# Building the next block's right factors inside the running block, by way of HBM, and last down weights in the up weights' buffers

## Chip, core and metric

The kernel runs on one core of a Trainium2 chip. The metric is the device time of one execution in microseconds (us), lower is better. Before the change it is 3266.54 us, the median of three runs (3254.4, 3266.54 and 3267.34).

The core's engines work side by side, each through its own instructions in order: TensorE (PE in the profile) multiplies matrices, VectorE (DVE) and GpSimd (POOL) do elementwise arithmetic, ScalarE (ACT) does activations and copies, and SyncE (SP) issues most transfers between HBM and the on-chip memory. They meet through semaphores.

## The reference, cut to the part that matters

One layer over 2048 tokens of width 1024 in float32: three token mixers side by side on a normalised input, a projection back that is added to `x`, and then a gated feed-forward part with a convolution of three taps over time. The change lies in the last line only.

```python
h = rms_norm(x, mix_norm_g[l])
...
x = x + jnp.concatenate([ya, yb, yc], axis=-1) @ w_out[l]
h = rms_norm(x, ffn_norm_g[l])
x = x + conv_glu_ffn(h, w_up[l], conv_w[l], conv_b[l], w_down[l])

def conv_glu_ffn(h, w_up, conv_w, conv_b, w_down):
    gate, val = jnp.split(h @ w_up, 2, axis=-1)
    gp = jnp.pad(gate, ((0, 0), (CONV_W - 1, 0), (0, 0)))
    conv = conv_b
    for i in range(CONV_W):
        conv = conv + gp[:, i:i + t] * conv_w[i]
    return (jax.nn.silu(conv) * val) @ w_down
```

`w_up` is 1024 x 5632 and `w_down` 2816 x 1024.

## The kernel before

The feed-forward part (lines 1246 to 1382) runs over three blocks of tokens, `BL`: 688, 680 and 680 tokens, each treated as two halves of n = 344 or 340 columns. Within a block a loop runs over the NF = 22 groups `fi` of 128 hidden units.

**Products in parts.** Every float32 matrix is split into a rounded high part and a rest (`split`, lines 142 to 144: a copy on ScalarE makes the high part, a subtraction on VectorE, or on GpSimd for down weights, the rest), and a product is three matmuls: high by high, high by rest, rest by high.

**Up projection.** `ffn_up` computes gate and value for both token halves by a scheme of seven products in the place of eight (Strassen's, in Winograd's form). The left factors are sums and differences of weight quarters: `up_w` loads two raw tiles of 512 KB (pool `raw`, three buffers), GpSimd makes four `S` tiles, and for each product ScalarE and VectorE split one left factor into a buffer `wu` (four buffers). The right factors, `Bs`, are seven tiles `B0` to `B6` made once for a block: `build` takes the rows j and j + 4 of `x` (eight rows of 128 features, scaled by two instructions of VectorE, line 1164), forms four sums and differences on GpSimd (lines 1169 to 1172) and splits seven tiles. Over j that is 8 scalings, 16 subtractions on GpSimd and 28 splits for a block. One product is 12 matmuls, a group `fi` 84. VectorE then adds seven results out of PSUM, two convolution taps (line 1314), the product with the value (line 1316) and the split of `hid`.

**Down projection.** After every second `fi` the two groups that are ready are multiplied by their down weights (`ffn_down`): 16 steps of six matmuls, and one addition into `acc` on VectorE for each (line 1338). Down weights (`down_w`) have two buffers `wd`, filled by a ScalarE copy and a GpSimd subtraction of 1024 columns.

**The end of a block.** After the last `fi` four groups are left: two rounds of down projection, 32 steps. The buffers of the right factors are free once the last up group has read them, so `build` for the next block stands here: one step of it after each of the 32 down steps (`PACE` = 1). The second round's down weights are loaded after the first round, into the same two buffers. Then `acc` is stored to the output, and the next block begins.

The order on each engine is made by a scheduler when the kernel is compiled. It takes instructions as its estimates say they become ready and buffers become free, in order of their place in the program where there is a choice. Raw weights, `x` rows, sums and results all go through SP's one order.

## Time and profile before

| | us |
|---|---|
| median of three runs | 3266.54 |
| the profiled execution | 3256.01 |
| its span, as the profile shows it | 3254.2 |
| TensorE busy | 3037.6 (93%) |
| VectorE busy | 2373.9 (73%) |
| ScalarE busy | 1399.3 (43%) |
| GpSimd busy | 1000.3 (31%) |

The feed-forward part begins at about 1815 us and holds some 1440 us. Matmuls are pipelined, so the durations of neighbouring ones overlap: a matmul row of 0.32 us follows the one before after some 0.16 us. Times in the rows count from the start of the span. A row that gives a wait names what came last before the engine went on.

### The profile page before, as it was taken

How to read it: one execution, taken by the hardware profiler on the slowest of the kernel's cores; microseconds unless marked ns; L12 is line 12 of the kernel's file. 1: busy time of each engine (PE TensorE's matmuls, PEld its weight loads, DVE VectorE, ACT ScalarE, POOL GpSimd, SP SyncE). 2: the span in 40 equal slices, each digit the busy share in tenths (PEclk: the TensorE clock that was granted, in tenths of full speed). 3: DMA queues.
4: the chain of work that ended last, by engine and by line, in shares of the span. 5: the costliest groups of instructions: out<-in, count | busy, mean ns of one | idle time of the engine just before them, and what ended most of it. 6: DMA issues, size and time to landing. Idle time of an engine off the chain costs nothing.

```text
span 3254.2 us, 49317 instructions
## 1 busy us (share of the span) xinstructions
PE 3037.6 (93%) x17820; PEld 2650.9 (81%) x17820; DVE 2373.9 (73%) x4569; ACT 1399.3 (43%) x2610; POOL 1000.3 (31%) x949
## 2 busy tenths in 40 slices
PE   6888899999999979999999999999899999999999
PEld 4567777776777755667699899999799998899999
DVE  5666666766677645677644688889988889988886
ACT  5343444434444334578733333333333334333332
POOL 3221001001000020144433444444544444444442
PEclk8888899999999987999999999999999999999999
DMA  7555665655653565532224422222422222422221
GB/s 222 148 166 170 175 181 163 190 149 157 162 161 101 169 152 141 141 99 77 76 90 148 143 79 78 78 78 74 154 74 77 78 78 81 140 78 78 78 79 67
DMA packets 440228, 392.94 MB, mean 121 GB/s; under 512 B 138809, under 2 KB 365637, under 8 KB 438633
## 3 DMA queue, kind: packets, MB, share of 16 engines
q1 hardware_dynamic: 435056, 377.99, 39.7%
q0 software_dynamic: 2816, 8.39, 0.9%
q10 hardware_dynamic: 2112, 3.41, 0.5%
q8 instruction: 141, 2.31, 0.3%
q14 instruction: 103, 0.84, 0.1%
HBM read 304.65 MB, written 86.36 MB: 120 GB/s over the span
## 4 chain that ended last, share of the span: by engine, by line
PE 66%; DVE 18%; issue 5%; ACT 4%; DMA 4%; POOL 2%; SPq 1%; POOLq 0%; ACTq 0%; DVEq 0%
PE ps L1291 7%; PE ps L1290 7%; PE ps L1289 7%; PE ps L1337 4%; PE ps L1335 4%; PE ps L1336 4%; PE mm L268 3%; PE mm L270 3%; PE mm L269 3%; DVE T L523 2%; PE o L1061 2%; DVE tm L520 2%; DVE wu L144 2%; PE z L639 2%; PE ps L1197 2%
## 5 line engine op out<-in xcount | busy, mean ns | idle before, releaser
L1291 PE MATMUL ps<-B,wu 128*128 128x340 f32 (+1 forms) x1848 | 593.2, 321 | 20.0 <-DVE wu L144 20.0
L1290 PE MATMUL ps<-B,wu 128*128 128x340 f32 (+1 forms) x1848 | 592.0, 320 | 0.0
L1289 PE MATMUL ps<-B,wu 128*128 128x340 f32 (+1 forms) x1848 | 589.4, 319 | 2.5 <-ACT wu L143 1.7
L1291 PEld LDWEIGHTS ps<-B,wu 128*128 128x128 f32 x1848 | 348.0, 188 | 27.6 <-DVE wu L144 27.2
L1335 PE MATMUL ps<-hid,wd 128*128 128x340 f32 (+1 forms) x1056 | 342.1, 324 | 14.3 <-ACT wd L143 10.2
L1289 PEld LDWEIGHTS ps<-B,wu 128*128 128x128 f32 x1848 | 347.9, 188 | 3.2 <-ACT wu L143 2.0
L1290 PEld LDWEIGHTS ps<-B,wu 128*128 128x128 f32 x1848 | 348.6, 189 | 0.1
L1337 PE MATMUL ps<-hid,wd 128*128 128x340 f32 (+1 forms) x1056 | 339.9, 323 | 3.1 <-POOL wd L144 3.0
L1336 PE MATMUL ps<-hid,wd 128*128 128x340 f32 (+1 forms) x1056 | 339.9, 322 | 0.0
L144 DVE TENSOR_TENSOR wu<-S,wu 128x512 fp32r<-128x512 f32 x264 | 257.0, 978 | 74.7 <-ACT wu L143 74.7
L1338 DVE TENSOR_TENSOR acc<-acc,ps 128x340 f32<-128x340 f32 (+1 forms) x528 | 248.3, 503 | 52.9 <-PE ps L1337 52.2
L144 POOL TENSOR_TENSOR wd<-raw,wd 128x1024 fp32r<-128x1024 f32 x66 | 171.0, 2613 | 277.3 <-ACT wd L143 272.9
L268 PE MATMUL mm<-hT,whi 128*128 128x512 f32 x520 | 235.9, 454 | 18.0 <-ACT whi L143 12.8
L270 PE MATMUL mm<-hT,wlo 128*128 128x512 f32 x520 | 220.3, 424 | 10.4 <-POOL wlo L144 6.4
L143 ACT CAST wu<-S 128x512 fp32r<-128x512 f32 x264 | 163.1, 619 | 150.5 <-PE ps L1291 137.9
L269 PE MATMUL mm<-hT,whi 128*128 128x512 f32 x520 | 219.3, 422 | 4.9 <-DVE hT L144 3.9
L1335 PEld LDWEIGHTS ps<-hid,wd 128*128 128x128 f32 x1056 | 201.8, 191 | 18.0 <-ACT wd L143 11.0
L144 DVE TENSOR_TENSOR wu<-raw,wu 128x512 fp32r<-128x512 f32 x198 | 203.0, 1026 | 6.4 <-ACT wu L143 6.4
L1337 PEld LDWEIGHTS ps<-hid,wd 128*128 128x128 f32 x1056 | 200.2, 190 | 5.5 <-POOL wd L144 5.5
L1336 PEld LDWEIGHTS ps<-hid,wd 128*128 128x128 f32 x1056 | 201.2, 190 | 0.0
L143 ACT CAST wu<-raw 128x512 fp32r<-128x512 f32 x198 | 121.5, 620 | 165.3 <-PE ps L1291 147.4
L268 PEld LDWEIGHTS mm<-hT,whi 128*128 128x128 f32 x520 | 105.5, 203 | 49.5 <-ACT whi L143 13.6
(348 smaller groups left out, 7140.4 us busy)
## 6 DMA issues: line engine op xcount, KB each, us to landing
raw<-in_w_up_dram SPq DMA_DIRECT2D x132, 512.0 KB
raw<-in_w_down_dram SPq DMA_DIRECT2D x66, 512.0 KB
whi<-whiD SPq DMA_DIRECT2D x48, 512.0 KB
wlo<-wloD SPq DMA_DIRECT2D x48, 512.0 KB
wraw<-in_w_in_dram SPq DMA_DIRECT2D x24, 512.0 KB
whiD<-whi SPq DMA_DIRECT2D x24, 512.0 KB
wloD<-wlo SPq DMA_DIRECT2D x24, 512.0 KB
xt<-in_xT_dram SPq DMA_DIRECT2D x48, 256.0 KB
```

The costliest lines, as they stand in the source:

```text
L143: (hi_eng or nc.scalar).copy(hi, src) if (hi_eng or nc.scalar) is nc.scalar else hi_eng.tensor_copy(out=hi, in_=src)
L144: (lo_eng or nc.vector).tensor_tensor(lo, src, f(hi), op=ALU.subtract)
L268: mm(ps, hi[:, kt, 0:P], hT[kt][:, 0, :], start=(kt == 0), stop=False)
L269: mm(ps, hi[:, kt, 0:P], hT[kt][:, 1, :], start=False, stop=False)
L270: mm(ps, lo[:, kt, 0:P], hT[kt][:, 0, :], start=False, stop=(kt == KT - 1))
L1289: mm(ps, whl[:, 0, kt, :], Bs[p][:, kt, 0, 0:n], start=(kt == 0), stop=False)
L1290: mm(ps, whl[:, 0, kt, :], Bs[p][:, kt, 1, 0:n], start=False, stop=False)
L1291: mm(ps, whl[:, 1, kt, :], Bs[p][:, kt, 0, 0:n], start=False, stop=(kt == 3))
L1335: mm(ps, wd[:, 0, ch], hid[:, 0, cs], start=(u == 0), stop=False)
L1336: mm(ps, wd[:, 0, ch], hid[:, 1, cs], start=False, stop=False)
L1337: mm(ps, wd[:, 1, ch], hid[:, 0, cs], start=False, stop=(u == G - 1))
L1338: nc.vector.tensor_tensor(acc[ct][:, cs], acc[ct][:, cs], ps, op=ALU.add)
```

## The change

`build` no longer writes into the `B` tiles itself; it hands each result to a function `put`. For block 0 this splits into the `B` tiles as before. For blocks 1 and 2 a new function, `build_ahead`, makes the factors while the block before runs: `put` splits into a staging tile `st` (pool `st4`, two buffers) and stores it to HBM (`kept`, seven tensors named `BD`), and the subtractions on GpSimd write `t` (four buffers of their own). Two steps of it are asked for after each `ffn_up` from fi = 2 on. At the block's end seven loads bring the factors back into the `B` tiles, in the order in which the products use them. The last two groups' down weights (`down_last`) are split into the four `wu` buffers in halves of 512 columns, so they need not wait for the `wd` buffers. A smaller scratch area for DMA descriptors makes room for the new tiles.

```diff
-    def build(Bs, b, src, tmp):
+    def build(put, b, src, tmp):
...
-                split(Bs[p][:, j, 0, 0:n], Bs[p][:, j, 1, 0:n], o)
+                put(p, j, o)
                 yield
...
+    def build_ahead(b):
+
+        t1, n1 = BL[b]
+        kept = [dram.tile([P, 4, 2, n1], F32, name=f"BD{b}{p}") for p in range(7)]
+
+        def load(kt):
+            xt = x4.tile([P, 2 * HN], F32, name="x4")
+            nc.sync.dma_start(out=xt[:, 0 : 2 * n1], in_=x2D[kt * P : (kt + 1) * P, t1 : t1 + 2 * n1])
+            return xt
+
+        def put(p, j, o):
+            t = st4.tile([P, 2, HN], F32R, name="st")
+            split(t[:, 0, 0:n1], t[:, 1, 0:n1], o)
+            nc.sync.dma_start(out=kept[p][:, j], in_=f(t[:, :, 0:n1]))
+
+        return kept, build(put, b, load, tmpB)
...
+    def down_last(fis):
+
+        raws = []
+        for fi in fis:
+            raw = raw4([P, DM])
+            nc.sync.dma_start(out=raw, in_=w_down[fi * P : (fi + 1) * P, :])
+            raws.append(raw)
+        whl = [[ws4.tile([P, 2, 4, P], F32R, name="wu") for _ in fis] for h in range(2)]
+        for u, raw in enumerate(raws):
+            for h in range(2):
+                t = whl[h][u]
+                split(t[:, 0], t[:, 1], raw[:, h * 512 : h * 512 + 512].rearrange("p (a c) -> p a c", c=P), None, nc.gpsimd)
+        return [lambda s, ct, u=u: whl[ct // 4][u][:, s, ct % 4, :] for u in range(len(fis))]
...
+        if b + 1 < len(BL):
+            kept, work = build_ahead(b + 1)
         for fi in range(NF):
             left = left_ if left_ is not None else up_w(fi)
             ready.append(ffn_up(Bs, left, fi, n))
+            for _ in itertools.islice(work, 2 if fi > 1 else 0):
+                pass
...
+        wdl = down_last(range(NF - G, NF))
         if b + 1 < len(BL):
...
             Bs = factors()
-            work = build(Bs, b + 1, load, tmp4)
+            for p in (0, 1, 6, 2, 3, 4, 5):
+                nc.sync.dma_start(out=f(Bs[p][:, :, :, 0 : BL[b + 1][1]]), in_=kept[p])
         while ready:
             for _ in ffn_down(acc, list(zip(ready, wds)), n):
-                for _ in itertools.islice(work, PACE):
-                    pass
+                pass
             ready = ready[G:]
-            if ready:
-                wds = [down_w(NF - G + u) for u in range(G)]
-        for _ in work:
-            pass
+            wds = wdl
...
-    nc = _bacc.Bacc("TRN2", target_bir_lowering=False, num_devices=1)
+    nc = _bacc.Bacc("TRN2", target_bir_lowering=False, num_devices=1, dynamic_dma_scratch_size=4096)
```

**How the instructions move.** TensorE's order is the same before and after but for the names of the last down weights. VectorE's is not. First the sixth up group of block 0 (fi = 5) on VectorE, before the change. `wu` are splits of up weights (from raw tiles or from `S`), `gt`, `u` and `vv` results taken out of PSUM (`ps`).

```order
L144 TENSOR_TENSOR wu_18193<-S_17977,wu_18193 128x512
L1299 TENSOR_TENSOR gt_18121<-u_18123,ps_18146 128x344
L144 TENSOR_TENSOR wu_18211<-S_17975,wu_18211 128x512
L144 TENSOR_TENSOR wu_18229<-S_17978,wu_18229 128x512
L1301 TENSOR_TENSOR u_18123<-u_18123,ps_18179 128x344
L144 TENSOR_TENSOR wu_18273<-raw_18256,wu_18273 128x512
```

The same place after the change. `st` is a staging tile, `x4` a row of `x`, `t` a sum from GpSimd; `rsb2` (the row statistics of block 2) tells that a scaling belongs to the build for block 2, the `st` tiles here belong to the build for block 1.

```order
L144 TENSOR_TENSOR st_20138<-x4_19837,st_20138 128x340
L144 TENSOR_TENSOR wu_18259<-S_18023,wu_18259 128x512
L1164 SCALAR_TENSOR_TENSOR x4_22520<-x4_22520,pps_61,rsb2_15189 128x680
L144 TENSOR_TENSOR wu_18277<-S_18026,wu_18277 128x512
L1326 TENSOR_TENSOR u_18171<-u_18171,ps_18227 128x344
L144 TENSOR_TENSOR wu_18343<-raw_18326,wu_18343 128x512
L144 TENSOR_TENSOR st_20142<-t_19842,st_20142 128x340
L1327 TENSOR_TENSOR u_18172<-u_18171,ps_18244 128x344
L144 TENSOR_TENSOR wu_18360<-raw_18326,wu_18360 128x512
L1328 TENSOR_TENSOR vv_18170<-u_18172,ps_18211 128x344
L144 TENSOR_TENSOR st_20293<-t_19843,st_20293 128x340
```

The scheduler moved both builds into block 0: all 56 splits and 16 scalings stand on VectorE between the first scaling, in the third up group (fi = 2), and the last split, in the down round after fi = 10. In that stretch of its order stand 66 splits of up weights and 72 down additions.

Second, VectorE in the second round of down projection at the end of block 0, before the change. `acc` are the additions of the down projection, `u_` sums from GpSimd, `B` the factors for block 1.

```order
L144 TENSOR_TENSOR B1_21587<-x4_21865,B1_21587 128x340
L1338 TENSOR_TENSOR acc3_17071<-acc3_17071,ps_21889 128x344
L144 TENSOR_TENSOR B2_21588<-u_21870,B2_21588 128x340
L1338 TENSOR_TENSOR acc4_17072<-acc4_17072,ps_21899 128x344
L144 TENSOR_TENSOR B3_21589<-u_21871,B3_21589 128x340
L1338 TENSOR_TENSOR acc4_17072<-acc4_17072,ps_21909 128x344
L144 TENSOR_TENSOR B4_21590<-u_21869,B4_21590 128x340
```

And after it, where `wu_22086` and `wu_22103` are the first two up weights of block 1.

```order
L1376 TENSOR_TENSOR acc3_17074<-acc3_17074,ps_21978 128x344
L144 TENSOR_TENSOR wu_22086<-raw_21752,wu_22086 128x512
L1376 TENSOR_TENSOR acc4_17075<-acc4_17075,ps_21986 128x344
L144 TENSOR_TENSOR wu_22103<-raw_21752,wu_22103 128x512
L1376 TENSOR_TENSOR acc4_17075<-acc4_17075,ps_21994 128x344
L1376 TENSOR_TENSOR acc5_17076<-acc5_17076,ps_22002 128x344
```

The splits of factors are gone from between the additions, and the first two up weights of the next block follow as soon as the first halves of the last down weights have been used.

Third, SP at the same end, after the change; `BD` are the factors kept in HBM. Before it, eight loads of `x` rows stood here, spread over the end.

```order
L1296 DMA raw_21752<-in_w_up_dram 128x1024
L1296 DMA raw_21754<-in_w_up_dram 128x1024
L1358 DMA raw_21764<-in_w_down_dram 128x1024
L1407 DMA B0_21780<-BD10_17087 128x8x340
L1407 DMA B1_21781<-BD11_17088 128x8x340
L1407 DMA B6_21786<-BD16_17093 128x8x340
L1358 DMA raw_21766<-in_w_down_dram 128x1024
L1407 DMA B2_21782<-BD12_17089 128x8x340
L1407 DMA B3_21783<-BD13_17090 128x8x340
```

The second raw down weight is issued behind three of the seven loads.

## Rows read from the trace of the kernel before

**Rows 1.** The page's first part: busy us of TensorE, its share of the span, instructions; then its weight loads (PEld) and the other engines.

```profile
PE 3037.6 (93%) x17820; PEld 2650.9 (81%) x17820; DVE 2373.9 (73%) x4569; ACT 1399.3 (43%) x2610; POOL 1000.3 (31%) x949
```

**Rows 2.** Busy time by stretch: start and end, length in us, then for PE, PEld, DVE, ACT and POOL busy us and instructions, the granted clock of TensorE as a share of the full one, the mean share of the DMA engines, GB/s. First the end of block 0, then the long stretch of block 1, then its end.

```profile
2262.00:2305.40 43.40, 34.77 (x193) 31.56 (x191) 40.51 (x66) 16.38 (x31) 21.80 (x20) 0.92 0.46 144
2350.00:2741.00 391.00, 389.39 (x2484) 388.38 (x2484) 337.56 (x491) 153.76 (x233) 179.60 (x135) 1.00 0.23 76
2741.20:2784.10 42.90, 35.47 (x194) 33.20 (x193) 40.02 (x66) 16.36 (x31) 22.30 (x20) 0.88 0.41 133
```

**Rows 3.** What TensorE's matmuls of the up projection waited for: total us, times, longest. One row each of four stretches, in this order: 2350 to 2741 (long stretch of block 1), 2305.4 to 2350 (start of block 1), 2784.1 to 2830 (start of block 2), 1850 to 2042 (192 us in block 0).

```profile
PE ps L1291 <- DVE wu L144: 1.6, 3, 0.8
...
PE ps L1291 <- DVE wu L144: 5.6, 5, 2.6
...
PE ps L1291 <- DVE wu L144: 5.0, 8, 1.2
...
PE ps L1291 <- DVE wu L144: 3.2, 3, 1.2
```

**Rows 4.** Single instructions in order of time: start us, duration us, engine, line, output and inputs, and in brackets the idle time before and what ended it. The first matmul of the end of block 0, the first of its second round, the first up matmul of block 1; the first of the end of block 1 and of block 2's ups; in the last end the first matmul, the first of the second round, and VectorE's last addition.

```profile
2261.97 0.31 PE L1335 MATMUL ps<-hid,wd 128*128 128x344 f32 x1
...
2284.52 0.65 PE L1335 MATMUL ps<-hid,wd 128*128 128x344 f32 x1 [4.71 <-ACT wd L143]
...
2305.45 0.42 PE L1289 MATMUL ps<-B,wu 128*128 128x340 f32 x1 [0.82 <-DVE acc L1338]
...
2741.24 0.32 PE L1335 MATMUL ps<-hid,wd 128*128 128x340 f32 x1
...
2784.14 0.37 PE L1289 MATMUL ps<-B,wu 128*128 128x340 f32 x1
...
3215.77 0.31 PE L1335 MATMUL ps<-hid,wd 128*128 128x340 f32 x1
...
3231.62 0.43 PE L1335 MATMUL ps<-hid,wd 128*128 128x340 f32 x1 [0.66 <-ACT wd L143]
...
3250.14 0.51 DVE L1338 TENSOR_TENSOR acc<-acc,ps 128x340 f32<-128x340 f32 x1 [0.41 <-PE ps L1337]
```

**Rows 5.** VectorE's scalings of `x` (line 1164) at the start of block 1, 2305.4 to 2350: count, shortest, median and longest duration in ns, first and last start.

```profile
L1164 DVE SCALAR_TENSOR_TENSOR x<-x,pps,rsb x3: 914/1949/1954, 2314.9 to 2334.5; 128x680 f32<-128x680 f32 x3
```

**Rows 6.** Busy time, as in rows 2, of 192 us in block 0.

```profile
1850.00:2042.00 192.00, 188.76 (x1189) 187.90 (x1188) 166.51 (x243) 73.17 (x110) 91.04 (x66) 1.00 0.22 75
```

**Rows 7.** VectorE's groups of instructions that build factors at the two ends, first 2262 to 2312, then 2741 to 2784: line, operation, output and inputs, shapes, count, busy us, mean ns of one, idle us before them. `u` are the sums from GpSimd.

```profile
L144 DVE TENSOR_TENSOR B<-u,B 128x340 fp32r<-128x340 f32 x16 | 13.7, 858 | 2.7 <-ACT B L143 2.7
L144 DVE TENSOR_TENSOR B<-x,B 128x340 fp32r<-128x340 f32 x11 | 10.0, 917 | 0.0
L1164 DVE SCALAR_TENSOR_TENSOR x<-x,pps,rsb 128x680 f32<-128x680 f32 x5 | 4.4, 913 | 0.0
...
L144 DVE TENSOR_TENSOR B<-u,B 128x340 fp32r<-128x340 f32 x14 | 10.9, 782 | 2.7 <-ACT B L143 2.7
L144 DVE TENSOR_TENSOR B<-x,B 128x340 fp32r<-128x340 f32 x10 | 7.3, 740 | 0.0
L1164 DVE SCALAR_TENSOR_TENSOR x<-x,pps,rsb 128x680 f32<-128x680 f32 x5 | 6.1, 1253 | 0.0
```

**Rows 8.** GpSimd at the end of block 0: the longest and the shortest of the four groups of sums for the factors, each of four instructions (columns as in rows 7), and then, in order of time (columns as in rows 4), the two subtractions that split down weights.

```profile
L1172 POOL TENSOR_TENSOR u<-u,x 128x340 f32<-128x340 f32 x4 | 4.9, 1221 | 0.0
...
L1171 POOL TENSOR_TENSOR u<-x 128x340 f32<-128x340 f32 x4 | 3.8, 962 | 3.3 <-DVE vv L1306 3.3
...
2284.55 4.96 POOL L144 TENSOR_TENSOR wd<-raw,wd 128x1024 fp32r<-128x1024 f32 x2 [1.53 <-ACT wd L143]
```

**Rows 9.** VectorE's instructions with both inputs in on-chip memory, in the long stretch 2350 to 2741: first by group with their means (columns as in rows 7), then shortest, median and longest of two of these groups (columns as in rows 5), and the same of one of GpSimd's four sums of up weights, over the whole feed-forward part.

```profile
L144 DVE TENSOR_TENSOR wu<-S,wu 128x512 fp32r<-128x512 f32 x77 | 73.9, 966 | 23.1 <-ACT wu L143 23.1
...
L144 DVE TENSOR_TENSOR wu<-raw,wu 128x512 fp32r<-128x512 f32 x57 | 59.3, 1040 | 2.0 <-ACT wu L143 2.0
...
L1314 DVE SCALAR_TENSOR_TENSOR cv<-gt,pps,cv 128x680 f32<-128x680 f32 x38 | 36.1, 951 | 4.7 <-ACT cv L1312 4.3
...
L144 DVE TENSOR_TENSOR hid<-cv,hid 128x680 fp32r<-128x680 f32 x20 | 27.9, 1393 | 2.3 <-ACT hid L143 2.3
...
L1316 DVE TENSOR_TENSOR cv<-cv,vv 128x680 f32<-128x680 f32 x19 | 25.1, 1322 | 0.0
...
L144 DVE TENSOR_TENSOR wu<-S,wu x77: 677/683/1962, 2351.8 to 2738.9; 128x512 fp32r<-128x512 f32 x77
...
L144 DVE TENSOR_TENSOR hid<-cv,hid x20: 866/1652/1964, 2350.0 to 2737.0; 128x680 fp32r<-128x680 f32 x20
...
L1276 POOL TENSOR_TENSOR S<-S,raw x66: 1286/1620/1929, 1813.9 to 3195.2; 128x512 f32<-128x512 f32 x66
```

**Rows 10.** Two splits of factors on VectorE in the end of block 0, in order of time (columns as in rows 4).

```profile
2283.73 0.50 DVE L144 TENSOR_TENSOR B<-u,B 128x340 fp32r<-128x340 f32 x1
...
2284.57 2.71 DVE L144 TENSOR_TENSOR B<-x,B 128x340 fp32r<-128x340 f32 x1
```

**Rows 11.** ScalarE's copies for these splits in the end of block 0 (columns as in rows 7).

```profile
L143 ACT CAST B<-u 128x340 fp32r<-128x340 f32 x16 | 7.6, 477 | 14.4 <-POOL u L1171 4.7 <-POOL u L1169 4.4 <-POOL u L1170 2.7
```

**Rows 12.** Transfers. First the main queue from 2284 to 2312: packets, MB, share of 16 engines. Then stores of another stage, issued by GpSimd: count, KB each, median us from issue to landing.

```profile
q1 hardware_dynamic: 2182, 5.64, 64.6%
...
yD<-yl POOLq DMA_DIRECT2D x16, 256.0 KB, 3.6
```

More of the change, by code (lines that the diff above doesn't have):

```diff
@@ L1218, in trunk_kernel, with put @@
                         Bs = factors()
-                        work = build(Bs, 0, lambda kt, done=done: done[kt], tmp3)
+                        def put(p, j, o, n=BL[0][1]):
+                            split(Bs[p][:, j, 0, 0:n], Bs[p][:, j, 1, 0:n], o)
+                        work = build(put, 0, lambda kt, done=done: done[kt], tmp3)
                 for _ in itertools.islice(work, WPACE):
@@ L1259, in trunk_kernel @@
     nc.vector.memset(gcar, 0.0)
+    st4 = p4.enter_context(tc.tile_pool(name="st4", bufs=2))
     G = 2
@@ L1264, in tmp4, with tmpB @@
         return u4.tile([P, HN], F32, name="u", tag="u")
+    def tmpB():
+        return st4.tile([P, HN], F32, name="t", tag="t", bufs=4)
+    def build_ahead(b):
[10 more added lines that the diff above has]
+        return kept, build(put, b, load, tmpB)
     def up_w(fi):
@@ L1325, in down_w @@
         split(wd[:, 0], wd[:, 1], raw, None, nc.gpsimd)
-        return wd
+        return lambda s, ct: wd[:, s, ct * P : (ct + 1) * P]
+    def down_last(fis):
[10 more added lines that the diff above has]
+        return [lambda s, ct, u=u: whl[ct // 4][u][:, s, ct % 4, :] for u in range(len(fis))]
     def ffn_down(acc, grp, n):
         for ct in range(KT):
-            ch = slice(ct * P, (ct + 1) * P)
             for hf in range(2):
@@ L1334, in ffn_down @@
                 for u, (hid, wd) in enumerate(grp):
-                    mm(ps, wd[:, 0, ch], hid[:, 0, cs], start=(u == 0), stop=False)
-                    mm(ps, wd[:, 0, ch], hid[:, 1, cs], start=False, stop=False)
-                    mm(ps, wd[:, 1, ch], hid[:, 0, cs], start=False, stop=(u == G - 1))
+                    mm(ps, wd(0, ct), hid[:, 0, cs], start=(u == 0), stop=False)
+                    mm(ps, wd(0, ct), hid[:, 1, cs], start=False, stop=False)
+                    mm(ps, wd(1, ct), hid[:, 0, cs], start=False, stop=(u == G - 1))
                 nc.vector.tensor_tensor(acc[ct][:, cs], acc[ct][:, cs], ps, op=ALU.add)
```

5 lines of the change are left out of this document (removed).

## The prediction

> **What bounds the kernel now.** I read the engine totals first, then the busy time by stage, then what TensorE waited for, then single instructions at the ends of the feed-forward blocks. TensorE is busy for 93% of the span of 3254.2 us [rows 1]. The profiled execution took 3256.0 us, 10.5 us under the median of 3266.5 of the runs shown, so the sum is made against 3256.0 and 10.5 is added at its end. The change touches the feed-forward part only, from about 1815 us on. The table by stage shows two kinds of stretches there [rows 2]. In the long ones (2350 to 2741 is one) TensorE is busy practically always and VectorE for 86%, and TensorE's waits come to 1.6 us in 391 [rows 3]. So TensorE is the bound there, with VectorE close behind. In the block ends it is not: they take 43.5, 42.9 and 34.4 us for 192 matmuls each, although 96 of them in a row, left alone, take 15.2 us, 0.158 each (3215.77 to 3230.96, that is 3231.62 less the wait of 0.66 in that row) [rows 4]. An undisturbed end is then 192 x 0.158 = 30.4 us.
>
> **What the change removes.** (a) At the ends of blocks 0 and 1 the splits of the next factors disappear from between the additions of the down projection. (b) The second pair of down weights no longer waits for the buffers of the first: 4.71 us in the first end [rows 4], with slow matmuls behind it (0.65 us in the same row, a granted clock of 0.92 and 0.88 over the two ends [rows 2]). From 2261.97 to 2305.45 it is 43.5 us, from 2741.24 to 2784.14 42.9 us [rows 4]; against 30.4 that is 13.1 + 12.5 = 25.6 us to win. The last end, from 3215.77 to its last addition at 3250.14, has 34.4 - 30.4 = 4.0 us, all by (b). (c) The first ups of blocks 1 and 2 wait 5.6 and 5.0 us for weight splits [rows 3]; VectorE still does three scalings for a coming build there, up to 1.95 us each [rows 5]. These go, but the new kernel enters the block with two up weights split instead of three, since the buffers hold down weights until then. Of the 10.6 us I take 3. **Gain: 25.6 + 4.0 + 3 = 32.6 us**, between 25 (the ends win 25, the starts nothing) and 36.
>
> **What it adds, and where.** The code asks for two build steps behind each up group of blocks 0 and 1. The order rows show something else: the scheduler puts the steps for block 2 right behind those for block 1. All 56 splits and 16 scalings so lie in block 0, in a stretch in which VectorE's order holds 66 splits of up weights and 72 down additions, thus TensorE 66 x 12 + 72 x 6 = 1224 matmuls, or 192 us. The other long stretches stay as they are. In 192 us of block 0 VectorE has 192 - 166.5 = 25.5 us free [rows 6]. The new work is priced by the same instructions in the block ends, where VectorE is as full as it will be here: 51 splits in 41.9 us, 0.82 each, and 10 scalings in 10.5 us, 1.05 each [rows 7]: 56 x 0.82 + 16 x 1.05 = 62.8 us, 37.3 more than fits. VectorE may run four up weights ahead of TensorE (four buffers of 12 matmuls, 7.5 us), which one dense stretch can use up once. **Loss: 37.3 - 7.5 = 30 us.** The lower end takes undisturbed rows, 0.50 us for a split [rows 10] and 0.91 for a scaling [rows 5]: 28 + 14.6 - 25.5 - 7.5 = 10 us. For the upper end GpSimd's 32 subtractions that come with it are counted too, 0.96 to 1.22 us each, together 34 us [rows 8]. Beside GpSimd's 180 us in 391 [rows 2], VectorE's splits of up weights take 0.97 and 1.04 us in the mean where 0.68 is the shortest, and its last product and last split 1.32 and 1.39 where 0.87 is [rows 9], some 62 us longer in all; 34 us more of GpSimd cost 12 in proportion, so 42 us.
>
> How the two engines meet shows in one pair of rows: a split that is 0.50 us long when undisturbed took 2.71 us when it began at 2284.57, 0.02 us behind two GpSimd subtractions of 4.96 us together [rows 8, 10]. The Trainium skill ("SBUF — State Buffer", section "Who interferes with whom") says that a VectorE instruction with two SBUF inputs and a GpSimd instruction that reads SBUF exclude one another for the whole instruction, whichever is first. This pair agrees. The scalings by convolution taps do not: they have two SBUF inputs and are still 0.95 us in the mean, 0.91 being the shortest of their size [rows 9, 5]. By the rule without exception the stretch needs both engines' times one after the other: 66 x 0.68 + 56 x 0.50 + 20 x 0.87 + 36 x 0.91 on VectorE, 38 x 1.29 + 9 x 2.48 + 34 on GpSimd, 228 us for 192 [rows 5, 8 to 10]: a loss of 36 us that no lead softens. That speaks against the change, and would put the time 6 us above my sum.
>
> **What I cost at nothing.** The 56 copies on ScalarE, 0.48 us each, 27 us in all [rows 11], fit: it is busy for 38% there [rows 6]; without that cover they would hold TensorE's weights one for one. The factors for each later block are 9.75 MB, stored in block 0 and read back at an end. At the rate of 28 us of the first end (5.64 MB, 201 GB/s, at a share of 64.6%, thus 312 GB/s at a full one [rows 12]) seven loads take 31 us. The first may start when product 0 of the last up group is done, 11 us before the down groups, and the last is needed 42 us into them; there are 53 us, so TensorE waits only below 184 GB/s. Among SP's loads the last raw down weight stands fourth; by the same rate it lands some 7 us into the first down group, which lasts 15. Splitting down weights in halves costs GpSimd what the whole ones cost. The smaller scratch for DMA descriptors touches transfers that GpSimd issues, long before.
>
> **Sum.** 3256.0 - 32.6 + 30 = 3253.4, on the scale of the median 3264. Forecast: no measurable change, which for this kernel means within 0.5%, or 16 us (the runs shown lie 13 us apart).
>
> **Rivals.** (1) *VectorE takes the splits cheaply; faster.* If they cost what undisturbed rows show, the loss is 10 us: 3256.0 - 32.6 + 10, on the median's scale 3244. For it: nearly all of VectorE's idle time in the long stretches is slack. Against it: GpSimd brings 34 us of its own into the same 192 us. (2) *The stores set the pace; slower.* Each step now ends in a store, from two staging buffers, and SP issues stores and weight loads in one order. ScalarE's copy into a staging buffer waits until the store before last has landed, and behind it on ScalarE stand copies of up weights that TensorE needs. A store of 340 KB lands in some 4.8 us (3.6 for 256 KB on another queue [rows 12], in proportion); with 0.48 + 0.82 us for copy and split a turn of two steps takes 6.1 us, 28 turns 171 of the 192 us. It decides once a turn exceeds 192 / 28 = 6.9 us: SP holding a store for 0.8 us, behind a raw load that waits for its buffer, is enough. At 1.8 us 28 x 1.0 us are lost beside the rest: 3264 + 28 = 3292. (3) *The ends do not get short*, because the loads run at half the rate: 9.75 MB at 150 GB/s are 65 us, 12 late at each of two ends: 3264 + 24 = 3288. Against it: the mean rate there, 201, is above that already, with a third of the share unused.
>
> **Chances.** The forecast, 3250 to 3280, has 0.44; rival 1 has 0.27, rival 2 0.22, rival 3 0.07. The range goes from rival 1 with 6 us more of gain or less of loss to rival 2 with 6 us more: 3238 to 3298. Faster by over 0.5% 0.27, within 0.44, slower 0.29.
>
> **What would show it.** Right: ends of 30 to 33 us at full clock; in block 0 TensorE's waits for weight splits grow from 3.2 us in 192 [rows 3] to some 30, with VectorE above 95%; the later long stretches unchanged. Rival 1: these waits stay under 15 us. Rival 2: SP and ScalarE wait for staging buffers, and TensorE for ScalarE's copies. Rival 3: TensorE waits for DMAs at the starts of blocks 1 and 2. A difference before 1815 us would prove the whole account incomplete.

## The result, and the profile after

The changed kernel takes **3282.6 us** (median of 9 runs, 3271.8 to 3293.6), the kernel before 3264.2 beside it: a ratio of **1.0066, 95% interval 1.0044 to 1.0087**. It is slower by some 20 us, more than a measurement's uncertainty; the forecast was no measurable change.

The feed-forward part, from its first up matmul to its last down matmul, tells it almost alone. It is 1431.2 us long in the profiled execution before and 1452.0 after. By pieces, each from TensorE's first matmul of a kind to its first of the next:

| us | before | after | difference | forecast |
|---|---|---|---|---|
| block 0, first up to the four last groups | 443.4 | 491.3 | +47.9 | +30 |
| ends of blocks 0, 1 and 2 | 43.4, 42.9, 34.0 | 30.4, 29.8, 29.8 | -30.3 | -29.6 |
| starts of blocks 1 and 2 (first up to first down) | 48.8, 46.5 | 48.8, 49.6 | +3.1 | -3 |
| blocks 1 and 2 from there to their ends | 387.0, 385.2 | 387.1, 385.2 | +0.1 | 0 |

The part before it lies apart: the profiled execution of the changed kernel enters the feed-forward part 14 us later (1832.8 against 1818.6 us). That turns out to be a difference between executions (first experiment).

Busy time by stage of the changed kernel; columns as in [rows 2]: stretch, its length, busy us (and instructions) of TensorE, weight loads, VectorE, ScalarE, GpSimd, then granted clock, DMA share and GB/s.

```profile
1884.10:2099.70 215.60, 185.84 (x1058) 174.13 (x1057) 199.15 (x276) 83.39 (x149) 114.79 (x87) 0.95 0.54 162
2324.10:2354.50 30.40, 30.40 (x193) 30.40 (x193) 20.81 (x40) 4.96 (x8) 5.69 (x6) 1.00 0.98 326
2354.50:2403.30 48.80, 41.35 (x255) 39.11 (x254) 40.38 (x45) 19.84 (x33) 26.05 (x18) 1.00 0.47 160
2403.30:2790.40 387.10, 385.91 (x2462) 385.09 (x2462) 333.28 (x489) 150.54 (x226) 175.23 (x133) 1.00 0.25 85
2790.40:2820.20 29.80, 29.80 (x194) 29.80 (x193) 20.45 (x40) 4.94 (x8) 5.68 (x6) 1.00 1.00 336
```

The second and the last line are the ends of blocks 0 and 1, which answer to [rows 2, 4]: TensorE is busy to the last tenth at full clock, while the factors come in at 326 and 336 GB/s. The fourth is the long stretch of block 1, unchanged. The first line is the one that pays: from the first down group of block 0 to its fifth, with 52 of the 56 splits in it, 215.6 us for what took 167.4 before (1870.3 to 2037.7); one split comes ahead of it and three behind. VectorE is busy for 199 of them, 92%, where the prediction's sign was above 95%. The rest of VectorE's time is waits; here are the waits of TensorE, VectorE and ScalarE in that stretch (what waited, for what; us in all, times, longest):

```profile
PE ps L1316 <- DVE wu L144: 25.2, 21, 4.3
PE ps L1314 <- ACT wu L143: 1.5, 2, 0.8
DVE st L144 <- ACT st L143: 9.2, 6, 3.4
DVE hid L144 <- ACT hid L143: 3.8, 4, 1.6
DVE wu L144 <- ACT wu L143: 2.3, 3, 1.0
DVE cv L1339 <- ACT cv L1337: 1.0, 1, 1.0
ACT st L143 <- DMA BD<-st: 107.1, 41, 8.5
```

TensorE waits for VectorE's weight splits, as the prediction said (it gave 3.2 us before [rows 3]). VectorE never waits for TensorE: its four lines are all waits for ScalarE, 9.2 + 3.8 + 2.3 + 1.0 = 16.3 us, and ScalarE waits 41 times for a staging buffer whose store hasn't landed. 199.2 + 16.3 is the whole stretch: VectorE, with its waits for ScalarE, sets its length. The costliest groups of VectorE there (shapes, count, busy, mean ns, idle before):

```profile
L144 DVE TENSOR_TENSOR wu<-S,wu 128x512 fp32r<-128x512 f32 x32 | 35.3, 1110 | 2.3 <-ACT wu L143 2.3
...
L144 DVE TENSOR_TENSOR st<-t,st 128x340 fp32r<-128x340 f32 x30 | 24.0, 801 | 6.8 <-ACT st L143 6.8
L144 DVE TENSOR_TENSOR st<-x,st 128x340 fp32r<-128x340 f32 x22 | 23.7, 1078 | 2.3 <-ACT st L143 2.3
...
L1164 DVE SCALAR_TENSOR_TENSOR x<-x,pps,rsb 128x680 f32<-128x680 f32 x14 | 15.3, 1091 | 0.1
```

A split costs 0.92 us in the mean (47.7 / 52) where I took 0.82, and a scaling 1.09 where I took 1.05 [rows 7].

At the start of block 1 the timeline of SP (the first three lines below) and of GpSimd (the last; start, length, operation, idle time before) shows what holds the start up now:

```profile
2353.36 2.22 SPq L1414 DMA_DIRECT2D out_dram<-acc  x2
2355.62 4.54 SPq L1384 DMA_DIRECT2D acc<-x2D  x5
2360.26 0.87 SPq L1296 DMA_DIRECT2D raw<-in_w_up_dram  x2
...
2368.20 1.29 POOL L1300 TENSOR_TENSOR S<-raw 128x512 f32<-128x512 f32 x1 [33.77 <-DMA raw<-in_w_up_dram]
```

The raw weights of the second up group are asked for behind the output stores and the new accumulators, 6 us into the block, and GpSimd has idled 34 us when it can make their sums, 13.7 us into the block. Before the change it made the first of them 7.3 us into the block (2312.79 - 2305.45):

```profile
2312.79 1.68 POOL L1275 TENSOR_TENSOR S<-raw 128x512 f32<-128x512 f32 x1 [2.74 <-DVE wu L144]
```

### The profile page after: what moved, and what is told of

Its sections match the earlier page's. It is cut to its first block, busy times and chain, and to the rows that moved or that the text cites. A ratio compares the mean times of both kernels' runs of the same rounds, so it can differ in the third digit from the quotient of the medians.

```text
span 3288.9 us, 49550 instructions
## 1 busy us (share of the span) xinstructions
PE 3059.2 (93%) x17820; PEld 2660.7 (81%) x17820; DVE 2380.7 (72%) x4569; ACT 1396.1 (42%) x2616; POOL 1009.8 (31%) x955
## 3 DMA queue, kind: packets, MB, share of 16 engines
q1 hardware_dynamic: 464848, 416.99, 42.9%
## 4 chain that ended last, share of the span: by engine, by line
PE 64%; DVE 18%; DMA 6%; ACT 4%; issue 4%; POOL 2%; SPq 1%; ACTq 0%; DVEq 0%; POOLq 0%
PE ps L1316 6%; PE ps L1315 6%; PE ps L1314 6%; PE ps L1373 5%; PE ps L1374 4%; PE ps L1375 4%; PE mm L268 3%; PE mm L269 3%; PE mm L270 3%; PE o L1061 2%; DVE T L523 2%; DVE wu L144 2%; DMA BD<-st 2%; DVE tm L520 2%; PE z L639 2%
## 5 line engine op out<-in xcount | busy, mean ns | idle before, releaser
L1316 PE MATMUL ps<-B,wu 128*128 128x340 f32 (+1 forms) x1848 | 599.3, 324 | 46.9 <-DVE wu L144 46.5
L1373 PE MATMUL ps<-hid,wd 128*128 128x340 f32 (+1 forms) x960 | 308.5, 321 | 1.9 <-DVE acc L1376 1.4
L1374 PE MATMUL ps<-hid,wd 128*128 128x340 f32 (+1 forms) x960 | 306.9, 320 | 1.0 <-DVE hid L144 1.0
L1375 PE MATMUL ps<-hid,wd 128*128 128x340 f32 (+1 forms) x960 | 306.7, 320 | 0.0
L268 PE MATMUL mm<-hT,whi 128*128 128x512 f32 x520 | 236.3, 454 | 17.1 <-ACT whi L143 12.7
L144 POOL TENSOR_TENSOR wd<-raw,wd 128x1024 fp32r<-128x1024 f32 x60 | 157.3, 2645 | 218.4 <-ACT wd L143 218.4
L144 DVE TENSOR_TENSOR wu<-raw,wu 128x512 fp32r<-128x512 f32 x198 | 196.1, 991 | 10.5 <-ACT wu L143 10.5
L1373 PEld LDWEIGHTS ps<-hid,wd 128*128 128x128 f32 x960 | 181.1, 189 | 5.9 <-DVE acc L1376 4.4
L1374 PEld LDWEIGHTS ps<-hid,wd 128*128 128x128 f32 x960 | 180.6, 188 | 1.5 <-DVE hid L144 1.2
L1375 PEld LDWEIGHTS ps<-hid,wd 128*128 128x128 f32 x960 | 180.6, 188 | 0.0
L1300 POOL TENSOR_TENSOR S<-raw 128x512 f32<-128x512 f32 x66 | 99.8, 1513 | 171.6 <-DMA raw<-in_w_up_dram 145.7
```

Source lines behind the costliest of these rows:

```text
L144: (lo_eng or nc.vector).tensor_tensor(lo, src, f(hi), op=ALU.subtract)
L268: mm(ps, hi[:, kt, 0:P], hT[kt][:, 0, :], start=(kt == 0), stop=False)
L1316: mm(ps, whl[:, 1, kt, :], Bs[p][:, kt, 0, 0:n], start=False, stop=(kt == 3))
L1373: mm(ps, wd(0, ct), hid[:, 0, cs], start=(u == 0), stop=False)
L1374: mm(ps, wd(0, ct), hid[:, 1, cs], start=False, stop=False)
L1375: mm(ps, wd(1, ct), hid[:, 0, cs], start=False, stop=(u == G - 1))
```

## The experiments

Two theories for the 48 us of block 0. **Overload:** VectorE's work is more than fits into the stretch into which the scheduler put it. **Stores** (rival 2 of the prediction): the two staging buffers hold ScalarE's copies, and these hold VectorE and TensorE. Later a third question came up, how much of it is GpSimd. All runs in one table; lengths are of the profiled executions, and the feed-forward part of the kernel before and of e1, which do the same there, agrees to 0.2 us. Blocks are counted from their first up matmul to their four last groups.

| run | ratio to before | feed-forward | block 0 | block 1 | block 2 | ends |
|---|---|---|---|---|---|---|
| before | 1 | 1431.2 | 443.4 | 435.8 | 431.7 | 43.4, 42.9, 34.0 |
| after | 1.0066 [1.0044, 1.0087] | 1452.0 | 491.3 | 435.9 | 434.8 | 30.4, 29.8, 29.8 |
| e1 scratch alone | 1.0000 [0.9988, 1.0013] | 1431.0 | 442.6 | 435.9 | 431.3 | 43.5, 42.8, 34.9 |
| e2 last down weights alone | 1.0006 [0.9991, 1.0021] | 1431.3 | 442.8 | 441.1 | 437.9 | 40.0, 39.7, 29.8 |
| e3 one build per block | 1.0044 [1.0026, 1.0061] | 1445.5 | 466.7 | 455.6 | 433.2 | 30.4, 29.8, 29.8 |
| e4 two steps behind each up group | 0.9992 [0.9976, 1.0008] | 1426.1 | 453.6 | 448.5 | 434.0 | 30.4, 29.8, 29.8 |
| e5 four staging buffers | 1.0050 [1.0031, 1.0070] | 1450.0 | 488.3 | 436.6 | 435.1 | 30.4, 29.8, 29.8 |
| e6 e4 with four staging buffers | 1.0000 [0.9982, 1.0019] | 1429.1 | 456.9 | 448.4 | 433.6 | 30.5, 29.9, 29.8 |
| e7 steps in the down groups | 0.9942 [0.9922, 0.9962] | 1408.7 | 444.8 | 440.2 | 433.8 | 30.4, 29.8, 29.8 |
| e8 e7, raw up weights first | **0.9898 [0.9874, 0.9922]** | 1403.2 | 444.4 | 438.0 | 430.8 | 30.4, 29.8, 29.8 |
| e9 after without GpSimd's sums | 1.0052 [1.0034, 1.0069] | 1440.1 | 481.6 | 434.7 | 433.8 | 30.4, 29.8, 29.8 |
| e10 after, sums on VectorE | 1.0063 [1.0038, 1.0088] | 1448.2 | 488.3 | 435.6 | 434.3 | 30.4, 29.8, 29.8 |
| e11 e8, sums on VectorE | 0.9925 [0.9904, 0.9945] | 1406.1 | 448.2 | 439.0 | 428.8 | 30.5, 29.8, 29.8 |
| e12 e9 with four staging buffers | 0.9990 [0.9971, 1.0009] | 1429.9 | 469.9 | 436.3 | 433.6 | 30.4, 29.9, 29.8 |

**e1, the smaller scratch alone**

```diff
-    nc = _bacc.Bacc("TRN2", target_bir_lowering=False, num_devices=1)
+    nc = _bacc.Bacc("TRN2", target_bir_lowering=False, num_devices=1, dynamic_dma_scratch_size=4096)
```

> The kernel before with the smaller DMA scratch (4096) and nothing else. The profiled execution of the changed kernel enters the feed-forward part 14 us later than that of the kernel before, and its first stage is 9 us longer. If the smaller scratch is the cause, this kernel shows it: the feed-forward part starts near 1833 us and the ratio is near 1.004. If it is a difference between two executions, the part starts near 1819 us as often as not and the ratio is within 0.1% of 1. The feed-forward part itself stays as before in both.

The ratio is 1.0000. Its feed-forward part began at 1829.8 us, between the two; over all profiled executions here it began anywhere from 1818.6 to 1840.2 (e2, which uses the old scratch), and with the changed kernel's scratch it also began at 1818.9 (e11) and 1821.0 (e10). So the 14 us are a difference between executions, and the change costs nothing ahead of the feed-forward part.

**e2, the last down weights alone**

```diff
+        wdl = down_last(range(NF - G, NF))
         if b + 1 < len(BL):
...
-            if ready:
-                wds = [down_w(NF - G + u) for u in range(G)]
+            wds = wdl
```

> Only the down weights of the last group go into the up factors' buffers; the next block's factors are still built in the block ends. By my terms the last end gains 4.0 us. In the first two ends the 4.71 us wait of TensorE goes, but VectorE still has 28 splits and 8 scalings to do there (some 31 us beside the additions), so the wait moves to the factors: between nothing and 5 us each. Together 4 to 10 us, ratio 0.997 to 0.9988. Rival: the buffers of the up factors are then given back late to the first up group of the next block, which costs as much as the ends gain; ratio 1.000 or above, the loss seen at the starts of blocks 1 and 2.

The rival was right. The ends gain 3.4, 3.2 and 4.2 us, and the starts of blocks 1 and 2 take 54.3 and 52.9 us instead of 48.8 and 46.5. The up weights' buffers hold down weights until the down groups have read them, so the next block begins without its first splits: before, VectorE had three of them done when the block began; in e2 it had none, and started the first 4.7 us later.

**e3, one set of kept factors**

```diff
+    keptD = [dram.tile([P, 4, 2, HN], F32, name=f"BD{p}") for p in range(7)]
+
     def build_ahead(b):
         t1, n1 = BL[b]
-        kept = [dram.tile([P, 4, 2, n1], F32, name=f"BD{b}{p}") for p in range(7)]
+        kept = [k[:, :, :, 0:n1] for k in keptD]
```

> The changed kernel with one set of kept factors in HBM for both later blocks: the build for block 2 can then not be moved into block 0, since its stores must wait until block 1's factors are loaded. Each of blocks 0 and 1 gets 28 splits and 8 scalings, still close together (some 6 up groups). If the loss is VectorE's work over what it has free, plus the waits for staging buffers, it is split over two blocks: block 0 some 24 us longer than before instead of 48, block 1 some 20 to 24 longer, and the sum unchanged: ratio 1.003 to 1.008. If VectorE's lead of four up weights and its free time take up half of the work in each block, the losses are 10 to 15 each and the ratio is 0.998 to 1.002. If the cost lay in the 9.75 MB of stores alone, block 0 and 1 share it in the same way, so this run does not separate that; it separates a loss that grows with the work in one stretch from one that is paid per step.

Blocks 0 and 1 are 23.3 and 19.8 us longer than before, 43.1 together: half of the work, half of the loss. That the scheduler drew both builds into one block was no harm by itself; that each of them is packed behind the first groups is.

**e4, two steps behind each up group**

```diff
-            for _ in itertools.islice(work, 2 if fi > 1 else 0):
-                pass
+            if fi > 1:
+                with tc.issue_after(lastv[0]):
+                    for _ in itertools.islice(work, 2):
+                        pass
```

(`lastv[0]` is VectorE's split of the hidden tile of this group; `issue_after` queues VectorE's instructions of the step behind it.)

> The changed kernel with its build steps held at two behind each up group (VectorE's part of a step is queued behind the split of that group's hidden tile), from group 2 to 15 in each of blocks 0 and 1. The work is the same, spread over some 600 us instead of 200. Overload theory (the loss is VectorE's work over its free time in one stretch): in a long stretch VectorE is busy for 86%, and 28 x 0.82 + 8 x 1.05 = 31 us fit into the 54 us that it has free in 390. Blocks 0 and 1 are then at most 5 us longer than before each, the ends stay at 30 us, and the sum is 20 to 30 us below the kernel before: ratio 0.991 to 0.994. Rival (each step costs TensorE time wherever it stands, by VectorE and GpSimd excluding each other or by the stores' waits in front of ScalarE's copies): the 48 us are still paid, 24 in each block, ratio 1.004 to 1.007. Half of it: near 0.999.

Of the 48 us, 22.9 are left (10.2 and 12.7): between the theories. The timeline of e4 shows one of these losses, in parts, ScalarE first, then VectorE, then TensorE:

```profile
2532.94 0.61 ACT L143 CAST wu<-raw 128x512 fp32r<-128x512 f32 x1
2535.28 0.48 ACT L143 CAST st<-x 128x340 fp32r<-128x340 f32 x1 [1.73 <-DVE x L1164]
2536.12 0.47 ACT L143 CAST st<-x 128x340 fp32r<-128x340 f32 x1 [0.36 <-DVE x L1164]
2536.50 1.13 ACT L143 CAST wu<-raw 128x512 fp32r<-128x512 f32 x2
...
2534.33 1.75 DVE L1164 SCALAR_TENSOR_TENSOR x<-x,pps,rsb 128x680 f32<-128x680 f32 x2
2536.01 0.50 DVE L144 TENSOR_TENSOR st<-x,st 128x340 fp32r<-128x340 f32 x1
...
2537.99 0.97 DVE L144 TENSOR_TENSOR wu<-S,wu 128x512 fp32r<-128x512 f32 x1
...
2539.01 0.42 PE L1316 MATMUL ps<-B,wu 128*128 128x340 f32 x1 [3.35 <-DVE wu L144]
```

Behind the split of a hidden tile VectorE owes TensorE weights at once. Two scalings and two build splits stand between it and the weight split that TensorE waits 3.35 us for. The rate is right here, the place is not.

**e5, four staging buffers in the changed kernel**

```diff
-    st4 = p4.enter_context(tc.tile_pool(name="st4", bufs=2))
+    st4 = p4.enter_context(tc.tile_pool(name="st4", bufs=4))
```

(and a scratch of 512, for room)

> The changed kernel with four staging buffers instead of two (and a scratch of 512 to make room; a scratch of 4096 for itself cost nothing). The order of the work stays as it was, with all 56 splits in the first stretch of block 0, which was 48 us longer than before. If VectorE's work is the bulk, only the waits behind stores go (16 us of VectorE's waits there): block 0 stays some 30 to 35 us longer than before, the feed-forward part some 5 us longer, ratio 1.001 to 1.003. If the stores set the pace (rival 2 of the prediction), most of the 48 us go: block 0 at most 10 us longer, feed-forward part 18 us or more shorter than before, ratio 0.995 or below. If neither is the cause of those waits, nothing changes: ratio 1.006.

Block 0 gets 3.0 us back and is still 44.9 us longer than before: more than the 30 to 35 of the first case, far from the 10 of the second. VectorE's waits and then its build instructions in the same four rounds of e5 (1871 to 2083):

```profile
DVE wu L144 <- ACT wu L143: 2.3, 2, 1.3
DVE hid L144 <- ACT hid L143: 2.0, 3, 1.3
DVE st L144 <- ACT st L143: 0.9, 2, 0.8
```

```profile
L144 DVE TENSOR_TENSOR st<-t,st 128x340 fp32r<-128x340 f32 x32 | 32.1, 1006 | 0.9 <-ACT st L143 0.9
...
L144 DVE TENSOR_TENSOR st<-x,st 128x340 fp32r<-128x340 f32 x23 | 19.7, 856 | 0.0
L1164 DVE SCALAR_TENSOR_TENSOR x<-x,pps,rsb 128x680 f32<-128x680 f32 x14 | 19.0, 1358 | 0.4 <-DMA x<-x2D 0.4
```

VectorE's waits for staging copies went from 9.2 to 0.9 us, all its waits from 16.3 to 6.0, and its instructions took the time. Splits of sums cost 1.01 us instead of 0.80 and scalings 1.36 instead of 1.09 (splits of the tiles themselves 0.86 instead of 1.08); in all it is busy for 6.5 us longer (205.7 us), some 3 us of it because 55 splits lie in the stretch and not 52. The stores theory falls as the cause of the 48 us, and my third case (the waits stay) as well.

**e6, e4 with four staging buffers.** The edits of e4 and e5.

> The paced kernel (two steps behind each up group) with four staging buffers. Paced alone left blocks 0 and 1 longer than before by 10 and 13 us. There ScalarE waits 38 us in 358 for staging buffers, and copies of up weights stand behind it. If that is what is left, blocks 0 and 1 come to within 4 us of before and the feed-forward part is some 20 us shorter than before: ratio 0.994. If it is the place of the steps (right behind a hidden tile, where VectorE owes TensorE the next up weights, and ScalarE's copy waits for VectorE's scaling), little changes: block 0 and 1 still 8 us or more longer each, ratio 0.998 to 1.000.

Blocks 0 and 1 are 13.5 and 12.6 us longer than before: nothing gained. So it isn't staging buffers that e4 still lacks; the place of its steps is left, which the next run moves.

**e7, the steps in the down groups**

```diff
-            for _ in itertools.islice(work, 2 if fi > 1 else 0):
-                pass
...
-                for _ in ffn_down(acc, list(zip(ready, wds)), n):
-                    pass
+                for k, add in enumerate(ffn_down(acc, list(zip(ready, wds)), n)):
+                    if k in (2, 6, 10) or (k == 14 and fi == G):
+                        with tc.issue_after(add):
+                            next(work, None)
```

(`add` is the addition of one down step.)

> The changed kernel with each build step queued on VectorE behind one addition of a down group (three steps in each of the nine steady down groups of blocks 0 and 1, four in the first), two staging buffers as before. In a down group VectorE has 16 additions of 0.43 us to do in 15.3 us and the next four up weights are split already, so it idles there for some 8 us; three steps are 3 x 0.82 + 1.05 = 3.5 us. Overload theory, with the place of the free time in it: blocks 0 and 1 as long as before within 3 us each, ends at 30 us, feed-forward part 22 to 30 us shorter: ratio 0.991 to 0.993. Rival (a step costs TensorE some 0.4 us wherever it stands): as paced, ratio 0.999.

Faster than before: 0.9942. Blocks 0 and 1 are 1.4 and 4.4 us longer than before (I had said within 3), with the same 56 splits, the same stores and two staging buffers. The feed-forward part is 22.5 us shorter.

**e8, e7 with the next raw up weights ahead of outputs and accumulators**

```diff
-        acc = [a4.tile([P, 2 * HN], F32, name=f"acc{ct}") for ct in range(KT)]
-        for ct in range(KT):
-            nc.sync.dma_start(out=acc[ct][:, 0 : 2 * n], in_=x2D[ct * P : (ct + 1) * P, ts_])
...
             left_ = up_w((fi + 1) % NF) if fi + 1 < NF or b + 1 < len(BL) else None
+            if fi == 0:
+                acc = load_acc()
```

(`load_acc` stores the block before, then loads the accumulators; both stood between the blocks.)

> As the one with the steps in the down groups, and at the starts of blocks 1 and 2 the raw weights of the second up group are asked for ahead of the output stores and the loads of the new accumulators. In the changed kernel these raw weights were asked for 6 us into the block and GpSimd idled 34 us for them; from the first up product to the first down product it took 48.8, 49.6 us where the steady pace would need some 40. If the late raw weights are the cause, the starts of blocks 1 and 2 get 3 to 8 us shorter each and the ratio is 0.002 to 0.004 below that of the run without this edit. Rival (the starts are bound by the chain of the first group's copies and splits after the buffers come free): no change in them.

0.9898 of before: some 33 us faster by the ratio, the best of all; 28.0 us of that show in the feed-forward part of the profiled execution. The starts take 46.2 and 45.6 us, 1.9 and 2.9 less than in e7; in e11, which has the same edit, they take 45.2 and 43.6, and in no version of the changed kernel without it less than 47.6. So the late raw weights were a cause, worth less than the 3 to 8 us that I said. At the pace of 0.158 us a matmul a start of 252 would take 39.8 us; the 6 us above that I didn't take apart. Three views of e8: the stages block 0 (from its first down group) and its end, VectorE's build instructions in block 0, and GpSimd's timeline at the start of block 1, which begins at 2311.4:

```profile
1886.40:2281.00 394.60, 391.52 (x2463) 389.07 (x2462) 349.52 (x525) 161.80 (x254) 203.85 (x149) 1.00 0.36 115
2281.00:2311.40 30.40, 30.40 (x193) 30.40 (x193) 20.88 (x40) 4.96 (x8) 5.69 (x6) 1.00 0.96 339
```

```profile
L144 DVE TENSOR_TENSOR st<-t,st 128x340 fp32r<-128x340 f32 x16 | 8.1, 505 | 2.9 <-ACT st L143 2.9
L1164 DVE SCALAR_TENSOR_TENSOR x<-x,pps,rsb 128x680 f32<-128x680 f32 x8 | 7.2, 919 | 0.0
L144 DVE TENSOR_TENSOR st<-x,st 128x340 fp32r<-128x340 f32 x12 | 6.1, 510 | 0.0
```

```profile
2313.41 1.29 POOL L1300 TENSOR_TENSOR S<-raw 128x512 f32<-128x512 f32 x1 [22.62 <-DVE wu L144]
```

In the down groups a split costs 0.51 us and a scaling 0.92, the undisturbed prices: 28 splits and 8 scalings make 8.1 + 7.2 + 6.1 = 21.4 us for a block, and they fit into time in which VectorE idled. In the last line GpSimd makes the first sum of the second up group 2.0 us after the block's first matmul (2311.4); in the changed kernel that was 13.7 us (2368.20 - 2354.5), before the change 7.3.

**e9, the changed kernel without GpSimd's sums in block 0**

```diff
+            if b:
+                t1, t2, t3, t4 = b12, b11, b21, b22
+            else:
...
```

> The changed kernel, its order kept, without GpSimd's 32 sums of the builds in block 0: the splits take the scaled tiles themselves (the four sums per step group are left out, so the factors of blocks 1 and 2 are other numbers). VectorE and ScalarE do the same instructions as in the changed kernel. Theory A (VectorE's own 56 splits and 16 scalings are what does not fit): GpSimd's 34 us only lengthen VectorE's instructions in proportion, by some 12 us, and block 0, 48 us longer than before in the changed kernel, is still 36 us longer; feed-forward part 1440 us, ratio 1.003. Theory B (an instruction of VectorE with two SBUF inputs and one of GpSimd exclude each other, and the sum of both engines is what does not fit): all 34 us of GpSimd come off, block 0 is some 10 to 18 us longer than before; feed-forward part 1418 to 1424 us, ratio 0.992 to 0.995.

Block 0 is 38.2 us longer than before instead of 47.9: theory A (36), not B (10 to 18). The feed-forward part, 1440.1 us, is theory A's too; the ratio, 1.0052, lies above its 1.003.

**e10, the same sums on VectorE**

```diff
+            eng = nc.vector if b else nc.gpsimd
...
-            nc.gpsimd.tensor_tensor(t3, b22, b12, op=ALU.subtract)
+            eng.tensor_tensor(t3, b22, b12, op=ALU.subtract)
```

> The changed kernel with the 32 sums of the builds in block 0 done by VectorE in place of GpSimd; all is computed. A sum there is as long as a split, 0.50 us undisturbed against 0.96 to 1.22 on GpSimd. Theory A (VectorE's own work is what does not fit): VectorE gets 32 x 0.5 to 0.8 = 16 to 26 us more and loses 12 of disturbance: block 0 is 52 to 62 us longer than before, feed-forward part 1456 to 1466 us, ratio 1.007 to 1.011. Theory B (both engines exclude each other, so that the sum of the two counts): 34 us of GpSimd become 16 of VectorE, block 0 is some 30 us longer than before, feed-forward part 1434 us, ratio 1.001.

44.9 us longer than before: between A (52 to 62) and B (30), and neither. Moving 32 sums from GpSimd to VectorE gains 3 us.

**e11, e8 with the sums on VectorE.** The edits of e8 and e10.

> The version with the steps in the down groups and the raw weights ahead, with the 32 sums on VectorE instead of GpSimd. What its blocks 0 and 1 still lose is 1.0 and 2.2 us. Theory B: the sums take less of the shared time, so these losses go and the feed-forward part, 1403 us, gets up to 3 us shorter: ratio 0.989. Theory A: VectorE has some 4 us left in a down group after the steps; the four sums of a step group are 2 to 3 us in one of them, which just fits: no change, or up to 5 us longer, ratio 0.990 to 0.9915.

0.9925; the feed-forward part is 2.9 us longer than in e8, within what theory A allowed; the ratio is 0.001 above its bound of 0.9915, less than the measurement's uncertainty. Moving the sums off GpSimd gains nothing here.

**e12, both edits of e5 and e9**

> The changed kernel's order with both edits at once: GpSimd's 32 sums in block 0 left out (the factors of blocks 1 and 2 are other numbers) and four staging buffers. Apart they gave back 9.7 us (no sums) and 3.0 us (four staging buffers) of the 47.9 that block 0 lost. If these two are separate terms, both together give back 13 and block 0 is still 35 us longer than before: feed-forward part 1437 us, ratio 1.002. If each took the other's place (with four buffers VectorE's waits went from 16 to 6 us in the first stretch, but its instructions got 6 us longer; without the sums they got shorter, but it still waited 19 us), both together give back far more: block 0 is 13 to 25 us longer, feed-forward part 1415 to 1427 us, ratio 0.990 to 0.997.

Block 0 is 26.5 us longer than before. Both together give back 21.4 us, where apart they gave 3.0 and 9.7. Two separate terms (35 left) are refuted; the second case (13 to 25) is missed by 1.5 us, and its ratio (0.990 to 0.997) by 0.002. Each of the two does take the other's place in part. Of the last 26.5 us the trace shows the kind: TensorE still waits 14.8 us for weight splits, while VectorE is busy for 194.5 of 200 us (97%) and waits for the other 5. That is the overload of the prediction, VectorE's own work over its free time. Its splits cost 0.71 us there and its scalings 1.30; how much of these prices is GpSimd's other work no run separates (e12, 1885 to 2085: busy time by engine, TensorE's wait, VectorE's groups):

```profile
1885.00:2085.00 200.00, 182.21 (x1088) 175.35 (x1087) 194.46 (x286) 83.62 (x149) 79.93 (x57) 0.97 0.61 183
```

```profile
PE ps L1319 <- DVE wu L144: 14.8, 14, 3.1
```

```profile
L144 DVE TENSOR_TENSOR st<-x,st 128x340 fp32r<-128x340 f32 x52 | 36.5, 708 | 0.0
...
L1164 DVE SCALAR_TENSOR_TENSOR x<-x,pps,rsb 128x680 f32<-128x680 f32 x14 | 18.2, 1302 | 2.9 <-DMA x<-x2D 2.9
```

## Why the prediction was wrong, by its own steps

**The gain at the ends was right:** 30.3 us for 29.6, at full clock. So were the loads of the factors: at the ends the transfers ran at 326 and 336 GB/s, and nothing waited. The long stretches of blocks 1 and 2 stayed as they were, and the two builds lay in block 0, as the order showed.

**The failed step is the loss in block 0, sized at 30 us and measured at 47.9.** Its first stretch can be added up from rows. VectorE there: 47.7 us of 52 splits and 15.3 of 14 scalings (I had 62.8 for all 56 and 16), 136.2 us of its other work (199.2 - 63.0), and 16.3 us of waits: 215.5 of the 215.6 us. In the same four rounds before, its work was 141.6 us (third number after the length):

```profile
1870.00:2037.00 167.00, 167.00 (x1056) 167.00 (x1055) 141.56 (x209) 64.40 (x96) 77.52 (x57) 1.00 0.23 76
```

VectorE's new work over its free time came out as predicted: 63.0 less 25.4 (167.0 - 141.6) is 37.6 us, and I had 37.3. In part that is luck: at my prices these 52 splits and 14 scalings come to 57.3 us, and the 5.7 us by which they were dearer stand in for the four splits and two scalings that lie outside the stretch. Two things were wrong:
- I gave VectorE 7.5 us of lead over TensorE, to be used up once. There was none to use. At the first down matmul of block 0 VectorE had split 21 up weights and TensorE had used 21, in both kernels; at the end of the stretch it is 77 and 77. VectorE gets four weights ahead in each down group of the stretch, in both kernels, and the ups behind it use them up, but for one or two before the change and to the last one after it.
- I took VectorE to work without a pause once it was full. It waited for ScalarE for 16.3 us, and ScalarE for stores. I had put this down as a rival to the overload, in which the stores set the pace. It came with the overload instead.

37.6 + 16.3, less 5.4 by which VectorE's other work got shorter, is 48.5; the stretch lost 215.6 - 167.4 = 48.2. But the waits aren't a term that can be taken away: with most of them gone (e5) VectorE's instructions were longer, and without GpSimd's sums (e9) the waits stayed. Only both edits together gave back 21 us, and left 26.5 of plain overload.

**GpSimd's share.** Leaving out GpSimd's sums (34 us by my price, 38.6 in the trace of the changed kernel) saved 9.7, near the 12 that I had in proportion [rows 8, 9]. By the sum of both engines' times the loss was 36 us, nearer to the result than my 30; but by it all 34 us would have come back in e9, and the loss would have fallen by some 18 us in e10, which measured 3. That sum came from the Trainium skill's rule in "SBUF — State Buffer", section "Who interferes with whom", that a VectorE instruction with two SBUF inputs and a GpSimd instruction that reads SBUF exclude one another for the whole instruction; taken as a sum of both engines' times it does not hold here. Single instructions do show that they meet: in the changed kernel the 26 build splits that overlap no GpSimd instruction take 0.505 us in the mean, the 30 others 1.25, and the six that begin during GpSimd's splits of down weights 2.54. Overlap alone does not set the price: in e8 29 of 56 overlap GpSimd's sums for the build or its small copies, and take 0.51.

**The starts, -3 us predicted, +3.1 measured.** The wait for weight splits did not go: it is 7.3 us at the start of block 1, where it was 5.6 [rows 3]. Behind it now stand the late raw weights, which SP asks for after outputs and accumulators; e8 moved them ahead and won 1.9 and 2.9 us. I counted the buffers that hold down weights and not the queue of transfers at that place.

**ScalarE's copies, costed at nothing:** its busy share was as I said (83 us of 216), but a copy that waits for a store stands in front of others. A busy share didn't show that.

**The forecast of no change** came from a balance of two terms of 30 us each, so that 18 us in one of them decided its sign. Rival 1 (cheap splits) failed in this order of the work, and yet e7 and e8 show its price, 0.51 us, where the steps stand in VectorE's idle time. Of rival 2's signs ScalarE's waits for stores came (107 us); TensorE's waits for ScalarE's copies hardly did (1.5 us), and with four staging buffers only 3.0 us came back. Rival 3 did not come.

## What to carry to other kernels

When work is moved off a stage's end into a stretch that "has room", find out where in each period the receiving engine idles and whom it owes next, and pin the work there: the same 56 splits cost 48 us where the scheduler packed them, 23 spread evenly at a bad place, and 6 in the down groups. Free time taken as a mean over a stretch tells neither. And waits and stretched instructions of a full engine replace each other, so a cause is weighed by removing both together as well as one at a time.

## What the runs showed of the hardware that was not expected

TensorE's granted clock fell after its waits in the packed stretch, from 1.00 to 0.50 of full, thus from 2.4 to 1.2 GHz. Four stretches of 5 us of the changed kernel:

```profile
2064.00:2069.00 5.00, 5.00 (x33) 5.00 (x33) 3.38 (x4) 3.61 (x6) 2.12 (x1) 1.00 0.48 146
2069.00:2074.00 5.00, 0.71 (x6) 0.42 (x4) 5.00 (x4) 2.04 (x4) 4.92 (x4) 0.84 0.49 126
2074.00:2079.00 5.00, 5.00 (x18) 5.00 (x19) 5.00 (x6) 0.95 (x3) 4.47 (x4) 0.50 0.67 223
2079.00:2084.00 5.00, 5.00 (x32) 4.87 (x31) 5.00 (x5) 1.15 (x3) 4.53 (x4) 0.98 0.22 77
```

In the second TensorE is busy for 0.71 us of 5, in the third it does 18 matmuls where 33 are usual. I take it to have cost nothing of its own here, since VectorE was busy for all of the last three stretches and waited for TensorE nowhere in the packed one; no run tried it. In the second stretch VectorE gets four instructions done in 5 us, beside four of GpSimd.
